# Keeping retention's rotated q on chip, turning y later, storing x1 by halves, and moving part of the last rotations to GpSimd

## The chip, the cores and the metric

The kernel runs on one core of one Trainium2 chip. Its time is the device time of one execution in microseconds (us); the figure for a kernel is the median of several executions. A profile is one more execution, recorded by the hardware; its span runs from the first to the last recorded event, and its own time, taken as for the other runs, is somewhat longer than the span.

The engines are named as in the profile: PE (TensorE, matmuls; PEld is its weight load), DVE (VectorE), ACT (ScalarE), POOL (GpSimd) and SP (SyncE, here only a queue that issues transfers). Each engine works through its instructions strictly in the order in which they were written into its queue, and waits at an instruction until the semaphores it names have come.

## The reference

One layer of a diffusion backbone over 1024 latent tokens (width 1024) with 256 context tokens. One input projection feeds two groups of heads; four heads do bidirectional chunkwise retention, four do differential attention.

```python
h_lat = rms_norm(x, norm1_g) * (1 + sc1) + sh1            # and h_ctx
rq, rk, rv, rg, dq, dk, dv = split(h @ w_in)               # rq, rk, dq, dk of the latents get a rotary embedding
# retention, forward and backward, per head, in chunks of 128
scores = einsum('bhid,bhjd->bhij', qc, kc) * intra
o = einsum('bhij,bhje->bhie', scores, vc) + einsum('bhid,bhde->bhie', qc * q_dec, S)
S = S * c_dec + einsum('bhjd,bhje->bhde', kc * k_dec, vc)
y_ret = silu(rg) * sum over both directions of head_group_norm(o)
# differential attention
a = softmax(s q1 k1) - lam * softmax(s q2 k2);  y_diff = subln(a @ v)
x = x + g1 * (concat([y_ret, y_diff]) @ w_out)
h2 = rms_norm(x, norm2_g) * (1 + sc2) + sh2
x = x + g2 * ((silu(a) * b) @ w_down)                      # a, b = split(conv3(h2 @ w_up))
out = rms_norm(x, final_g)
```

## The kernel before, in words

**Passes.** Every projection product is made of three matmul passes over high and low parts of the operands (`passes`, L131 to L133). The tile `pl` is such a product: 24 matmuls of 128x512, eight steps of three. After each step `tick()` advances a generator that runs beside the projection and writes the instructions of another piece of work between the passes. `beside(gen, rate, start)` sets it: `rate` steps of the generator for each tick, beginning with a debt of `start`.

**Stages.** To about 75 us: modulation vectors, first norm, transposes. Then the column blocks of w_in one after another: dv, dk, retention's v, its k, the silu gate (with the states of heads 0 and 1 beside it), q (block 0, from about 327 us), dq (block 4, eight tiles of 512 columns: two halves `hf` of each of four heads). Beside q and dq runs `outputs()`, which does retention's outputs. The last three dq tiles (`TAIL = 3`) are run beside the first attention units. Attention lasts to about 665 us, the output projection with the second norm to about 755 us, the up and down projections to the end.

**A rotation** (`rotated`, L413 to L426) takes one `pl` tile out of PSUM: ACT writes the two halves of the rows, swapped, to `xb` (L416, two instructions), DVE forms `xa = pl * cos` (L418), `xb = xb * sin` (L419) and `xa = xa + xb` (L420). A q or k tile is then stored to DRAM (L425, `rqk_d`, 256 KB); a dq or dk tile goes through `split_store`: ACT casts the high part (L408), DVE subtracts it for the low part (L409), and a store takes both (L410).

**Retention's outputs.** A `Pair` is two chunks of 128 tokens of one head; there are 16. In iteration n of `outputs()`, pair n + 2 is made, which issues the load of its rotated q and k from DRAM (`qk`, L242, 256 KB). `score` of pair n issues the load of v and the gate (`kvo`, L227), forms q times its decay on POOL (`qq`, L249), and q by k on PE (`pc`, L252, four matmuls); DVE multiplies with the decay mask (`sc`, L254). `output` accumulates `po` on PE from `kvo`, `sc`, the state `S` and `qq` (L260, L261) and ACT copies it out (L265). `squares` takes sums of squares on ACT (L269), POOL a power (L271), DVE scales `o` (L276), POOL adds the directions and multiplies with the gate (`y`, L278, L279: the last reader of `kvo`). `turn` transposes y on PE (`pyt`, L284), ACT and DVE split it (L286, L287) and SP stores it (`yrd`, L289). Pair n is turned in iteration n + 2.

**Entry to attention.** When the last y is done, POOL issues the loads of the first units' queries (`qhl`, L940), keys (`ks`, L943) and values (`va`, L946). A unit's scores `pA` (L861) are reduced by DVE (`mt`, the row minimum, L864), exponentiated by ACT (`p`, L868), combined by DVE (L876) and transposed by PE (`pt`, L881). The steps in `EARLY` of the first two units are set between the passes of the last three dq tiles.

**The output projection** goes over the column halves n = 0, 1 and within each over the eight token tiles t. DVE forms `gated` (L1123) and adds x (L1124). After n = 1, `norm2(t)` stores the sum `x1[t]` to DRAM (`x1d`, L1068, 512 KB), ACT squares it (L1070), and DVE scales it in place (L1074). SP also carries the first loads of w_up (`wra`, `wrb`, L1040) in this stage.

**What sets the order.** The instructions are written in program order as above and a scheduler of the framework then orders each engine's queue; the pools give each tile a number of buffers (`bufs`), and a new tile waits until the last reader of the buffer it takes is done.

Of the kernel before, what the change touches and what calls it, by code (L numbers as in the profile page):

```python
# [8 lines left out]
F32 = mybir.dt.float32  # L9
# [3 lines left out]
ALU = mybir.AluOpType  # L13
# [4 lines left out]
P = 128  # L18
D = 1024
KD = D // P  # L20
L = 1024
# [5 lines left out]
H = 4  # L27
# [5 lines left out]
RET_SCALE = 128.0 ** -0.5  # L33
DIFF_SCALE = 64.0 ** -0.5
# [26 lines left out]
TAIL = 3  # L61
# [6 lines left out]
def r32(ap):  # L68
    return ap.bitcast(F32)
# [3 lines left out]
def kernel(  # L73
# [58 lines left out]
        mm(ps, lh, rl, start=False, stop=False, skip_group_check=more)  # L132
        mm(ps, ll, rh, start=False, stop=last, skip_group_check=more)  # L133

    rqk_d = [dr.tile([P, 2, L], F32, name=f"rqk{h}") for h in range(H)]
    kvg_d = [dr.tile([P, H, 3, 2, P], F32, name=f"kvg{g}") for g in range(NKT // 2)]
    g1_d = dr.tile([P, D], F32, name="g1d")
    g2_d = dr.tile([P, D], F32, name="g2d")
# [15 lines left out]
    with ExitStack() as p1:  # L154
# [68 lines left out]

        def load_kv(h, g, nm, s0):

            kv = rt.tile([P, 2, 2, P], F32, name=nm, bufs=3 + (s0 == 0))
            nc.sync.dma_start(out=kv, in_=kvg_d[g][:, h, s0 : s0 + 2])  # L227
            return kv

# [6 lines left out]
        class Pair:  # L236


            def __init__(self, n):
                self.h, self.g = divmod(n, NT // 2)  # L240
                self.qk = rt.tile([P, 2, 2, P], F32, name="qk")
                nc.sync.dma_start(out=self.qk, in_=rqk_d[self.h][:, :, 2 * self.g * P : (2 * self.g + 2) * P].rearrange("p i (s l) -> p i s l", s=2))  # L242

            def score(self):
                kv = load_kv(self.h, self.g + 1, "kvo", 1)
                self.v, self.sg = kv[:, 0], kv[:, 1]
                over = [P, 2, 2, P]
                self.qq = rt.tile(over, F32, name="qq")
                nc.gpsimd.tensor_tensor(out=self.qq, in0=self.qk[:, 0].unsqueeze(2).to_broadcast(over), in1=qd[:, self.h].unsqueeze(1).to_broadcast(over), op=ALU.mult)  # L249
                pc = tr_tile([P, 2, P], "pc2")  # L250
                for s in range(2):
                    mm(pc[:, s, :], self.qk[:, 1, s, :], self.qk[:, 0, s, :], start=True, stop=True)  # L252
# [38 lines left out]
        states_at, last_y = {}, []  # L291

        def states(heads):

# [43 lines left out]
        def outputs():  # L338
            n_pairs, per_head = H * NT // 2, NT // 2
            pairs, more = {}, states((2, 3))  # L340
            for n in range(-2, n_pairs + 2):
                if n + 2 < n_pairs:
                    pairs[n + 2] = Pair(n + 2)
                if n == -2:
                    continue
                if n + 1 < n_pairs:
                    pairs[n + 1].score()
                forming = per_head <= n < 3 * per_head
                if n == per_head - 1 or forming and n % 2 == 0:
                    next(more)  # L350
                yield
                if 0 <= n < n_pairs:
                    pairs[n].output(0)
                yield
                if forming:
                    next(more)
                yield
                if 0 <= n < n_pairs:
                    pairs[n].output(1)
                    pairs[n].squares()  # L360
                yield
# [40 lines left out]

            return fin

        def split_store(src, dst):
            n = src.shape[-1]
            hl = ev.tile([P, 2, 512], F32R, name="xhl")
            nc.scalar.copy(hl[:, 0, :n], src)  # L408
            nc.vector.tensor_tensor(out=hl[:, 1, :n], in0=src, in1=r32(hl[:, 0, :n]), op=ALU.subtract)  # L409
            nc.sync.dma_start(out=dst.rearrange("p m a l -> (p m) a l"), in_=r32(hl[:, :, :n]))  # L410

        def rotated(pt, dst, rtab, blk, scale, col0, h, hf):
            xa = ev.tile([P, 512], F32, name="xa")  # L413
            xb = ev.tile([P, 512], F32, name="xb")
            for q in (0, 64):
                nc.scalar.activation(xb[q : q + 64, :], pt[64 - q : P - q, :], AF.Copy, scale=scale)  # L416
            cs, sn = rtab[hf][:, 0, :], rtab[hf][:, 1, :]
            nc.vector.scalar_tensor_tensor(out=xa, in0=pt, scalar=scale, in1=cs, op0=ALU.mult, op1=ALU.mult)  # L418
            nc.vector.tensor_tensor(out=xb, in0=xb, in1=sn, op=ALU.mult)  # L419
            nc.vector.tensor_tensor(out=xa, in0=xa, in1=xb, op=ALU.add)  # L420
            c0 = col0 + hf * 512
            if blk == 32:
                split_store(xa, dst[h][:, :, :, c0 : c0 + 512])
            else:
                nc.sync.dma_start(out=dst[h][:, c0 : c0 + 512], in_=xa)  # L425
            return xa  # L426

# [9 lines left out]
        def transposed(wget, dst, rtab, blk, scale, col0, order, nat=False):  # L437
            todo = None
            for h, hf in order:
                pt = mm_tile("pl")  # L440
                for k in range(KD):
                    passes(pt, wget(k, h * P, (h + 1) * P), tuple(hT[a][hf][:, k, :] for a in range(2)), k == 0, k == KD - 1)
                    tick()
                    if todo and k == KD - 2:
                        natural_copy(*todo)
                xa = rotated(pt, dst, rtab, blk, scale, col0, h, hf)
                todo = (xa, h, hf) if nat else None
            if todo:
                natural_copy(*todo)
# [372 lines left out]
        transposed(wg, [q[:, 1] for q in rqk_d], rtab, 64, RET_SCALE, 0, by_head, True)  # L822
        wg = stream_block(3)
        psbS.close()
        psb2 = psx.enter_context(ExitStack())
# [239 lines left out]
        nc.sync.dma_start(out=x1[t], in_=x[t * P : (t + 1) * P, :])  # L1065

    def norm2(t):
        nc.sync.dma_start(out=x1_d[t], in_=x1[t])  # L1068
        sq = xo.tile([P, D], BF16, name="sq2")
        nc.scalar.activation(sq, x1[t], AF.Square, accum_out=sm2[:, t : t + 1])  # L1070
        rsqrt(sm2[:, t : t + 1], sm2[:, t : t + 1], 1.0 / D, EPS, 1)
        if t == 0:
            nc.scalar.activation(sm2[:, 32:33], sm2[:, 0:1], AF.Silu)
        nc.vector.tensor_scalar(out=x1[t], in0=x1[t], scalar1=sm2[:, t : t + 1], scalar2=None, op0=ALU.mult)  # L1074

    def turned(hf, d, raw, on_act):
        pt = pst.tile([P, 512], F32, name="pt3", tag="tr")
# [32 lines left out]
    with ExitStack() as p3:  # L1110
        ps = p3.enter_context(tc.tile_pool(name="ps3", bufs=2, space=PSUM))
        for n in range(2):
            sl = wo_first if n == 0 else []
            for _ in wo_gen if n == 0 else out_weights(n, sl):
                pass
            for t in range(NT):
                pt = ps.tile([P, 512], F32, name="po3", tag="mm")
                for k in range(KD):
                    passes(pt, tuple(yT[a][t // 4][:, k, t % 4 * P : (t % 4 + 1) * P] for a in range(2)), sl[k], k == 0, k == KD - 1)
                    tick()  # L1120
                dst = x1[t][:, n * 512 : (n + 1) * 512]
                gated = wo.tile([P, 512], F32, name="gated")
                nc.vector.tensor_tensor(out=gated, in0=pt, in1=g1[:, n * 512 : (n + 1) * 512], op=ALU.mult)  # L1123
                nc.vector.tensor_tensor(out=dst, in0=gated, in1=dst, op=ALU.add)  # L1124
                if n == 1:
                    norm2(t)
                    if t == 1:
                        pre = [raw_load("wra" if j < 2 else "wrb", w_up[j]) for j in range(NPRE)]
                        early = [[split_op(a[:, c : c + 4, :]) for c in (0, 4)] for a in pre]
                        raws = [up_load(j) for j in range(NSUM)]  # L1130
                        for a, b in raws:
                            sums_in_place(a, b)
                    if t == 3:
                        beside(turned0(), 0.5, -3.0)
        beside(iter(()), 0.0)
# [495 lines left out]
```

## Time and the profile before

| | |
|---|---|
| median of 3 runs | 1394.26 us (1393.91 to 1397.99) |
| profiled execution: its own time | 1398.66 us |
| profiled execution: span | 1396.9 us |
| mean granted clock of PE | 0.997 |
| busy in the span | PE 1365.7 us (98%), DVE 1003.0 (72%), ACT 729.6 (52%), POOL 296.9 (21%) |
| chain that ended last | PE 86%, DMA 5%, DVE 4%, ACT 2%, issue 2%, POOL 1% |

The page of the profile lists busy time by engine, the span in 40 slices of about 35 us, the transfers, the chain of work that ended last, and the costliest groups of instructions. The waits view lists for an engine the instruction that waited, the one that released it, the sum in us, the count and the longest. In a timeline row the numbers are the start, the duration, the engine, line and operation, and in square brackets the idle time of the engine before it and what ended it.

### The profile page before, as it was taken

Reading aid. Unit: us, or ns where it says so; the run is one execution under the profiler, and the core shown is the slowest. Engines: PE = TensorE matmul, PEld = TensorE weight load, DVE = VectorE, ACT = ScalarE, POOL = GpSimd, SP = SyncE. Lnnn points to the kernel's source line nnn. Section 1 sums busy time; section 2 is a strip of 40 time slices with the busy share of each in tenths; the row PEclk is TensorE's granted clock in tenths of the full one; section 3 lists DMA queues with packets and bytes.
Section 4 is the critical chain, followed back from the end, with each engine's and each line's share of the span. In section 5 each row is a group of like instructions: output and inputs, shape, how many; then the busy total and the mean of one; then the engine's idle time right before and its main releaser. Section 6 shows DMA issues by size and latency. Waiting matters only on the chain.

```text
span 1396.9 us, 19447 instructions
## 1 busy us (share of the span) xinstructions
PE 1365.7 (98%) x7038; PEld 1146.9 (82%) x7038; DVE 1003.0 (72%) x1462; ACT 729.6 (52%) x1395; POOL 296.9 (21%) x321
## 2 busy tenths in 40 slices
PE   8999999999999899999999999999999999999997
PEld 5788888888887799998888788888888888888886
DVE  4655773424676798896347998777788777798757
ACT  4652222424575689997126645555445555454543
POOL 1310000001556133421201732233332220000001
PEclk9999999999999999999999999999999999999999
DMA  9546885465574696641421223323233225963523
GB/s 360 211 166 216 286 277 175 142 174 164 178 237 141 181 222 155 127 97 46 166 84 61 91 106 114 113 91 113 100 111 113 85 81 177 374 232 99 181 91 128
DMA packets 96807, 218.81 MB, mean 157 GB/s; under 512 B 9220, under 2 KB 31236, under 8 KB 96200
## 3 DMA queue, kind: packets, MB, share of 16 engines
q1 hardware_dynamic: 87976, 190.83, 40.0%
q0 software_dynamic: 8160, 24.91, 7.9%
q10 hardware_dynamic: 576, 1.84, 0.4%
q8 instruction: 55, 0.90, 0.3%
q14 instruction: 40, 0.33, 0.1%
HBM read 160.13 MB, written 57.41 MB: 156 GB/s over the span
## 4 chain that ended last, share of the span: by engine, by line
PE 86%; DMA 5%; DVE 4%; ACT 2%; issue 2%; POOL 1%; SPq 0%; POOLq 0%; ACTq 0%; DVEq 0%
PE chain L131 5%; PE chain L133 5%; PE chain L132 5%; PE pv L893 5%; PE c L132 5%; PE pA L861 5%; PE c L131 5%; PE c L133 5%; PE pn L131 4%; PE pn L133 4%; PE pn L132 4%; PE pl L133 3%; PE pl L131 3%; PE pl L132 3%; PE third L131 3%; PE third L133 3%
## 5 line engine op out<-in xcount | busy, mean ns | idle before, releaser
L131 PE MATMUL pl<-hT,whi 128*128 128x512 f32 x256 | 106.5, 416 | 0.0
L131 PE MATMUL chain<-T,whi 128*128 128x512 f32 x264 | 103.2, 392 | 0.7 <-ACT ua L1177 0.4
L132 PE MATMUL chain<-T,whi 128*128 128x512 f32 x264 | 102.8, 389 | 0.0
L133 PE MATMUL chain<-T,wlo 128*128 128x512 f32 x264 | 102.4, 389 | 0.0
L133 PE MATMUL pl<-hT,wlo 128*128 128x512 f32 x256 | 100.6, 393 | 0.0
L132 PE MATMUL pl<-hT,whi 128*128 128x512 f32 x256 | 100.4, 392 | 0.0
L864 DVE TENSOR_REDUCE mt<-pA 128x1 f32<-128x1280 f32 x64 | 95.3, 1490 | 3.7 <-PE pA L861 3.3
L861 PE MATMUL pA<-ks,qhl 128*128 128x512 f32 (+1 forms) x384 | 89.5, 369 | 3.0 <-ACT p L868 2.7
L133 PE MATMUL c<-whi,ghl 128*128 128x512 f32 x232 | 90.3, 389 | 0.0
L131 PE MATMUL c<-whi,ghl 128*128 128x512 f32 x232 | 90.3, 389 | 0.0
L132 PE MATMUL c<-wlo,ghl 128*128 128x512 f32 x232 | 90.3, 389 | 0.0
L868 ACT ACTIVATE p<-pA,mt 128x1280 f32<-128x1280 f32 x64 | 85.5, 1335 | 6.8 <-DVE mt L864 6.7
L1032 ACT CAST whi<-cmb 128x512 fp32r<-128x512 f32 x62 | 38.5, 622 | 81.1 <-PE chain L132 60.7
L861 PEld LDWEIGHTS pA<-ks,qhl 128*128 128x128 f32 x384 | 67.6, 189 | 15.2 <-ACT p L868 3.4
L893 PE MATMUL pv<-va,aT 128*128 128x128 f32 x640 | 76.9, 275 | 0.1
L131 PE MATMUL pn<-whi,hT 128*128 128x512 f32 x188 | 76.8, 409 | 0.0
L133 PE MATMUL pn<-whi,hT 128*128 128x512 f32 x188 | 73.8, 393 | 1.3 <-POOL hT L548 1.2
L1035 DVE TENSOR_TENSOR wlo<-cmb,whi 128x512 fp32r<-128x512 f32 x62 | 60.3, 974 | 20.3 <-ACT whi L1032 20.3
L1191 POOL TENSOR_TENSOR cmb<-wrb 128x512 f32<-128x512 f32 x19 | 27.8, 1462 | 221.1 <-DMA wrb<-w_up 132.0
L893 PEld LDWEIGHTS pv<-va,aT 128*128 128x128 f32 x640 | 74.0, 192 | 0.7 <-DVE yT L922 0.3
L132 PE MATMUL pn<-wlo,hT 128*128 128x512 f32 x188 | 73.7, 392 | 0.8 <-DVE wlo L571 0.8
L1032 ACT CAST whi<-wra 128x512 fp32r<-128x512 f32 x55 | 33.7, 622 | 72.8 <-PE third L132 42.5
(319 smaller groups left out, 3822.5 us busy)
## 6 DMA issues: line engine op xcount, KB each, us to landing
wm<-w_mod SPq DMA_DIRECT2D x32, 512.0 KB, 5.3
raw<-w_in SPq DMA_DIRECT2D x27, 512.0 KB, 4.6
wra<-w_up SPq DMA_DIRECT2D x24, 512.0 KB, 3.3
wrb<-w_up SPq DMA_DIRECT2D x22, 512.0 KB, 3.6
W<-w_down SPq DMA_DIRECT2D x44, 256.0 KB, 5.3
ad<-s SPq DMA_DIRECT2D x20, 512.0 KB, 3.5
wra<-ad SPq DMA_DIRECT2D x20, 512.0 KB, 3.7
kvs<-kvg SPq DMA_DIRECT2D x36, 256.0 KB, 3.1
```

Of the source, the lines that this page charges most:

```text
L131: mm(ps, lh, rh, start=first, stop=False, skip_group_check=more)
L132: mm(ps, lh, rl, start=False, stop=False, skip_group_check=more)
L133: mm(ps, ll, rh, start=False, stop=last, skip_group_check=more)
L861: mm(self.pa[m][:, c0:c1], self.q[:, m, i, qs], self.k[:, m, c0:c1], start=(i == 0), stop=(i == 1))
L864: nc.vector.tensor_reduce(out=self.mt[:, m : m + 1], in_=self.pa[m][:, :LK], axis=AX.X, op=ALU.min)
L868: nc.scalar.activation(self.p[m], self.pa[m][:, :LK], AF.Exp, scale=-1.0, bias=self.mt[:, m : m + 1], accum_out=self.s[:, m : m + 1])
L893: mm(self.pv, self.aT[:, c, :], self.v[:, c, :], start=(c == 0), stop=(c == NKT - 1))
L1032: cast = nc.scalar.copy(hi, src)
L1035: nc.vector.tensor_tensor(out=lo, in0=src, in1=r32(hi), op=ALU.subtract)
L1191: nc.gpsimd.tensor_tensor(out=s1, in0=b1, in1=b2, op=ALU.add)
```

## The change

Four edits are made together.

1. **q stays in SBUF.** `rotated` is called with no destination for block 0. The result stays in its tile (`turned_q[h, hf]`: an `st` buffer for the first half of a head, the `xa` buffer for the second), and `score` reads q from there. The eight q stores of 256 KB are gone. What a pair loads is k alone (`rk`, 128 KB in place of `qk`, 256 KB). The `kvo` load moves from `score` to the making of the pair, two pairs earlier, and `kvo` has four buffers, not three.
2. **y is turned in iteration n + 3**, in the middle of the iteration, not n + 2 at its end. The loop is one iteration longer, and the start debt is 16 rather than 18.
3. **x1 is stored by halves** of 512 columns, each right after its own add, and the scaling of the second norm is done as two instructions of 512 columns.
4. **In the last three dq tiles** the product with the sine and the low-part subtraction run on POOL.

```diff
-    rqk_d = [dr.tile([P, 2, L], F32, name=f"rqk{h}") for h in range(H)]
+    rk_d = [dr.tile([P, L], F32, name=f"rk{h}") for h in range(H)]
...
-            kv = rt.tile([P, 2, 2, P], F32, name=nm, bufs=3 + (s0 == 0))
+            kv = rt.tile([P, 2, 2, P], F32, name=nm, bufs=4)
...
-                self.qk = rt.tile([P, 2, 2, P], F32, name="qk")
-                nc.sync.dma_start(out=self.qk, in_=rqk_d[self.h][:, :, 2 * self.g * P : (2 * self.g + 2) * P]...)
-
-            def score(self):
+                self.k = rt.tile([P, 2, P], F32, name="rk")
+                nc.sync.dma_start(out=self.k, in_=rk_d[self.h][:, 2 * self.g * P : (2 * self.g + 2) * P]...)
                 kv = load_kv(self.h, self.g + 1, "kvo", 1)
                 self.v, self.sg = kv[:, 0], kv[:, 1]
+
+            def score(self):
+                o = self.g % 2 * 2 * P
+                q = turned_q[self.h, self.g // 2][:, o : o + 2 * P].rearrange("p (s l) -> p s l", s=2)
...
-                    mm(pc[:, s, :], self.qk[:, 1, s, :], self.qk[:, 0, s, :], start=True, stop=True)
+                    mm(pc[:, s, :], self.k[:, s, :], q[:, s, :], start=True, stop=True)
...
-            for n in range(-2, n_pairs + 2):
+            for n in range(-2, n_pairs + 3):
...
+                if 0 <= n - 3 < n_pairs:
+                    pairs[n - 3].turn()
                 if 0 <= n < n_pairs:
                     pairs[n].output(1)
...
-                if 0 <= n - 2 < n_pairs:
-                    pairs[n - 2].turn()
                 yield
...
-            nc.vector.tensor_tensor(out=hl[:, 1, :n], in0=src, in1=r32(hl[:, 0, :n]), op=ALU.subtract)
+            eng.tensor_tensor(out=hl[:, 1, :n], in0=src, in1=r32(hl[:, 0, :n]), op=ALU.subtract)
...
-            xa = ev.tile([P, 512], F32, name="xa")
+            if dst is None and hf == 0:
+                xa = ev.tile([P, 4, P], F32, name="st").rearrange("p h e -> p (h e)")
+            else:
+                xa = ev.tile([P, 512], F32, name="xa")
+            if dst is None:
+                turned_q[h, hf] = xa
...
-            nc.vector.tensor_tensor(out=xb, in0=xb, in1=sn, op=ALU.mult)
+            eng.tensor_tensor(out=xb, in0=xb, in1=sn, op=ALU.mult)
             nc.vector.tensor_tensor(out=xa, in0=xa, in1=xb, op=ALU.add)
...
-        beside(outputs(), 1.35, -18.0)
-        transposed(wg, [q[:, 0] for q in rqk_d], rtab, 64, 1.0, 0, by_head)
+        beside(outputs(), 1.35, -16.0)
+        transposed(wg, None, rtab, 64, 1.0, 0, by_head)
...
-        transposed(wg, dq_d, rtab, 32, -DIFF_SCALE, 0, by_head[-TAIL:])
+        transposed(wg, dq_d, rtab, 32, -DIFF_SCALE, 0, by_head[-TAIL:], eng=nc.gpsimd)
...
     def norm2(t):
-        nc.sync.dma_start(out=x1_d[t], in_=x1[t])
...
-        nc.vector.tensor_scalar(out=x1[t], in0=x1[t], scalar1=sm2[:, t : t + 1], scalar2=None, op0=ALU.mult)
+        for c in (0, 512):
+            nc.vector.tensor_scalar(out=x1[t][:, c : c + 512], in0=x1[t][:, c : c + 512], scalar1=sm2[:, t : t + 1], scalar2=None, op0=ALU.mult)
...
                 nc.vector.tensor_tensor(out=dst, in0=gated, in1=dst, op=ALU.add)
+                nc.sync.dma_start(out=x1_d[t][:, n * 512 : (n + 1) * 512], in_=dst)
```

In the changed kernel the same code has other line numbers: the load of k is L242, the score matmuls `pc` are L254, `po` L262 and L263, the rotation L425 to L427, the subtraction L411, `mt` L871, the store of x1 L1132, the loads of w_up L1047.

The first scores of retention on PE, before: two `pc` of two pairs and all eight `po` of a pair stand close together, 61 `pl` passes into block 0.

```order
L131 MATMUL pl<-hT_167,whi 128x512
L252 MATMUL pc_2925<-qk 128x128 x2
L132 MATMUL pl<-hT_169,whi 128x512
L133 MATMUL pl<-hT_167,wlo 128x512
L252 MATMUL pc_2957<-qk 128x128 x2
L260 MATMUL po<-kvo,sc 128x128
L261 MATMUL po<-S_2463,qq 128x128
L260 MATMUL po<-kvo,sc 128x128
L261 MATMUL po<-S_2464,qq 128x128
L260 MATMUL po<-kvo,sc 128x128
```

The same place on PE after; `st` is the kept q. The upper piece is the first `pc`, the lower one begins 13 passes behind it.

```order
L133 MATMUL pl<-hT_170,wlo 128x512
L254 MATMUL pc_2920<-st,rk 128x128 x2
...
L133 MATMUL pl<-hT_167,wlo 128x512
L254 MATMUL pc_2954<-st,rk 128x128 x2
L262 MATMUL po<-kvo,sc 128x128
L263 MATMUL po<-S_2463,qq 128x128
L262 MATMUL po<-kvo,sc 128x128
L263 MATMUL po<-S_2464,qq 128x128
L131 MATMUL pl<-hT_167,whi 128x512
```

The first `pc` now stands 39 passes into block 0 (15 behind the end of the first q tile), the second 15 passes later, and the eight `po` are in two groups with six passes between them.

On DVE at the entry to attention, before: the rotations of the last dq tiles with the reductions `mt` of the first units between them.

```order
L419 TENSOR_TENSOR xb<-xb,rtab_3723 128x512
L864 TENSOR_REDUCE mt<-pA 128x1
L420 TENSOR_TENSOR xa<-xa,xb 128x512
L872 RECIPROCAL r<-sa 128x1
L409 TENSOR_TENSOR xhl<-xa,xhl 128x512
L864 TENSOR_REDUCE mt<-pA 128x1 x2
L873 SCALAR_TENSOR_TENSOR r<-r,sa,nlam 128x1
L876 SCALAR_TENSOR_TENSOR p_4275<-p_4273,r,p_4275 128x1280
L864 TENSOR_REDUCE mt<-pA 128x1
```

On DVE after:

```order
L425 SCALAR_TENSOR_TENSOR xa<-pl,rtab_3740 128x512
L871 TENSOR_REDUCE mt<-pA 128x1
L879 RECIPROCAL r<-sa 128x1
L427 TENSOR_TENSOR xa<-xa,xb 128x512
L425 SCALAR_TENSOR_TENSOR xa<-pl,rtab_3739 128x512
L871 TENSOR_REDUCE mt<-pA 128x1 x2
L427 TENSOR_TENSOR xa<-xa,xb 128x512
L880 SCALAR_TENSOR_TENSOR r<-r,sa,nlam 128x1
L883 SCALAR_TENSOR_TENSOR p_4267<-p_4265,r,p_4267 128x1280
L871 TENSOR_REDUCE mt<-pA 128x1
```

The product with the sine (before L419) and the subtraction (before L409) of these tiles have left DVE. They stand on POOL, behind the loads of the first units; on POOL after:

```order
L953 DMA va<-dvd 128x10x128
L426 TENSOR_TENSOR xb<-xb,rtab_3740 128x512
L947 DMA qhl<-dq_85 64x4x512
L411 TENSOR_TENSOR xhl<-xa,xhl 128x512
L426 TENSOR_TENSOR xb<-xb,rtab_3739 128x512
L947 DMA qhl<-dq_85 64x4x512
L411 TENSOR_TENSOR xhl<-xa,xhl 128x512
```

So L427 on DVE waits for L426 on POOL, and the reductions queued behind L427 on DVE wait with it.

On SP in the output projection the order after is as follows; before, no `x1d` stood ahead of these loads of `wra` and `wrb`, and all eight came as whole tiles behind `woraw`.

```order
L1132 DMA x1d_94<-x_0_6682 128x512
L1047 DMA wrb<-w_up 128x1024
L1132 DMA x1d_95<-x_1_6683 128x512
L1047 DMA wra<-w_up 128x1024
L1047 DMA wrb<-w_up 128x1024
L1047 DMA wra<-w_up 128x1024
L1132 DMA x1d_96<-x_2_6684 128x512
L1047 DMA wrb<-w_up 128x1024
```

More of the change, by code (lines that the diff above doesn't have):

```diff
@@ L289, in turn @@
                 nc.sync.dma_start(out=yr_d[self.g // 2][:, :, self.h, o : o + 2 * P].rearrange("p a (s l) -> p a s l", s=2), in_=r32(yr))
-        states_at, last_y = {}, []
+        states_at, last_y, turned_q = {}, [], {}
         def states(heads):
@@ L403, in store_to, with split_store @@
             return fin
-        def split_store(src, dst):
+        def split_store(src, dst, eng=nc.vector):
             n = src.shape[-1]
@@ L408, in split_store, with rotated @@
             nc.scalar.copy(hl[:, 0, :n], src)
-            nc.vector.tensor_tensor(out=hl[:, 1, :n], in0=src, in1=r32(hl[:, 0, :n]), op=ALU.subtract)
+            eng.tensor_tensor(out=hl[:, 1, :n], in0=src, in1=r32(hl[:, 0, :n]), op=ALU.subtract)
             nc.sync.dma_start(out=dst.rearrange("p m a l -> (p m) a l"), in_=r32(hl[:, :, :n]))
-        def rotated(pt, dst, rtab, blk, scale, col0, h, hf):
-            xa = ev.tile([P, 512], F32, name="xa")
+        def rotated(pt, dst, rtab, blk, scale, col0, h, hf, eng=nc.vector):
+            if dst is None and hf == 0:
[4 more added lines that the diff above has]
+                turned_q[h, hf] = xa
             xb = ev.tile([P, 512], F32, name="xb")
@@ L422, in rotated @@
             if blk == 32:
-                split_store(xa, dst[h][:, :, :, c0 : c0 + 512])
-            else:
+                split_store(xa, dst[h][:, :, :, c0 : c0 + 512], eng)
+            elif dst is not None:
                 nc.sync.dma_start(out=dst[h][:, c0 : c0 + 512], in_=xa)
@@ L435, in natural_copy, with transposed @@
                 nc.sync.dma_start(out=kvg_d[1 + 2 * hf + i][:, h, 0], in_=st[:, 2 * i : 2 * i + 2, :])
-        def transposed(wget, dst, rtab, blk, scale, col0, order, nat=False):
+        def transposed(wget, dst, rtab, blk, scale, col0, order, nat=False, eng=nc.vector):
             todo = None
@@ L445, in transposed @@
                         natural_copy(*todo)
-                xa = rotated(pt, dst, rtab, blk, scale, col0, h, hf)
+                xa = rotated(pt, dst, rtab, blk, scale, col0, h, hf, eng)
                 todo = (xa, h, hf) if nat else None
@@ L821 @@
         rt = rtx.enter_context(tc.tile_pool(name="rt", bufs=2, side="right"))
-        transposed(wg, [q[:, 1] for q in rqk_d], rtab, 64, RET_SCALE, 0, by_head, True)
+        transposed(wg, rk_d, rtab, 64, RET_SCALE, 0, by_head, True)
         wg = stream_block(3)
```

4 lines of the change are left out of this document (2 added, 2 removed).

## The prediction

> **What bounds the kernel now.** I read the summary of busy time first, then the list of waits for PE, then the busy time stage by stage, and last the chain and the timeline at the few places where PE stood still.
>
> ```profile
> PE 1365.7 (98%) x7038; PEld 1146.9 (82%) x7038; DVE 1003.0 (72%) x1462; ACT 729.6 (52%) x1395; POOL 296.9 (21%) x321
> ```
>
> PE works for 98% of the span, so the only time to be had without removing matmuls is its idle time, 1396.9 - 1365.7 = 31.2 us. The change removes no matmul. The waits of PE (sum in us, count, longest) tell which part of those 31 us it can reach:
>
> ```profile
> PE pc L252 <- DMA qk<-rqk: 4.5, 3, 1.6
> PE pA L861 <- ACT p L868: 2.7, 2, 1.7
> PE po L260 <- DMA kvo<-kvg: 1.9, 1, 1.9
> ...
> PE pu L326 <- ACT jk L269: 1.0, 1, 1.0
> ...
> PE pt L881 <- DVE xa L418: 0.9, 1, 0.9
> PE pyt L284 <- POOL y L279: 0.4, 1, 0.4
> PE pA L861 <- DMA ks<-dk: 0.3, 1, 0.3
> ```
>
> All seven lie in retention and at the entry to attention. By stage (stretch, length, busy time of PE, PEld, DVE, ACT, POOL, then the granted clock):
>
> ```profile
> 350.00:400.00 50.00, 46.85 (x314) 41.98 (x313) 34.06 (x80) 30.89 (x101) 27.44 (x30) 1.00 0.65 204
> 400.00:450.00 50.00, 46.15 (x269) 39.47 (x268) 35.63 (x77) 28.97 (x96) 29.20 (x31) 0.97 0.52 171
> 450.00:500.00 50.00, 46.10 (x263) 39.37 (x263) 38.21 (x50) 32.14 (x62) 11.91 (x23) 1.00 0.78 187
> ...
> 700.00:800.00 100.00, 99.26 (x466) 80.91 (x465) 73.44 (x115) 54.00 (x89) 28.46 (x17) 1.00 0.22 82
> 800.00:1300.00 500.00, 500.00 (x2204) 412.95 (x2203) 412.40 (x493) 260.41 (x382) 106.97 (x79) 1.00 0.39 135
> ```
>
> From 350 to 500 us PE idles 10.9 us, nowhere behind it does it idle as much: from 800 to 1300 it has no idle time at all, and what is saved ahead of it moves the end by as much.
>
> **The q kept in SBUF.** The chain shows how q reaches PE before:
>
> ```profile
> 331.18 2.53 DMA rqk<-xa
> 333.72 3.87 DMA qk<-rqk
> 337.63 0.71 PE pc L252 x4
> ...
> 351.06 3.76 DMA qk<-rqk
> ...
> 363.50 5.69 DMA qk<-rqk
> 369.32 0.68 PE pc L252 x4
> ```
>
> A store of 2.5 us and a load of 3.8 to 5.7 us stand between the rotation and the scores, and the three waits of `pc` are these loads. Afterwards `pc` needs a tile that DVE has just written and a `rk` that was stored long before (k is rotated two column blocks earlier). The 4.5 us go. What is late next is the rotation itself:
>
> ```profile
> 333.36 1.20 ACT L416 ACTIVATE xb<-pl 64x512 f32<-64x512 f32 x2 [4.26 <-PE pl L133]
> 334.59 0.69 DVE L418 SCALAR_TENSOR_TENSOR xa<-pl,rtab 128x512 f32<-128x512 f32 x1 [3.44 <-ACT xb L416]
> ...
> 335.92 0.69 DVE L420 TENSOR_TENSOR xa<-xa,xb 128x512 f32<-128x512 f32 x1
> ...
> 331.12 0.39 PE L131 MATMUL pl<-hT,whi 128*128 128x512 f32 x1
> 331.35 0.39 PE L132 MATMUL pl<-hT,whi 128*128 128x512 f32 x1
> ```
>
> From the end of the product to the rotated tile it takes 336.61 - 333.36 = 3.25 us. In the new order 15 passes stand between the end of the first q tile and the first `pc`; passes start 331.35 - 331.12 = 0.23 us apart, so they cover 3.4 us, some 0.2 us less than rotation and two handovers at most. I put the new wait at 0.2 us, its ends at 0 and 0.7 (one DVE instruction late). Later pairs have several tiles' time. The balance of this part is -4.5 + 0.2 = -4.3 us.
>
> **The earlier load of v and gate, and the clock.** At 427 us SP stands at the `kvo` load, because its buffer is read by `y` of an earlier pair on POOL, and PE stands behind it:
>
> ```profile
> 427.45 4.39 SPq L227 DMA_DIRECT2D kvo<-kvg  x2
> ...
> 431.31 0.46 PE L260 MATMUL po<-kvo,sc 128*128 128x128 f32 x2 [1.89 <-DMA kvo<-kvg]
> ...
> 432.70:436.10 3.40, 3.40 (x13) 3.03 (x12) 2.32 (x6) 0.90 (x2) 1.48 (x3) 0.50 0.43 149
> 436.10:440.00 3.90, 3.90 (x23) 3.32 (x22) 1.62 (x3) 2.28 (x11) 2.78 (x3) 1.00 0.38 146
> ```
>
> Issued two iterations ahead and into a fourth buffer, the load has two iterations to land: eighteen iterations share the time from the first `pc` at 337 us to the entry to attention at about 450, 6 us each, so 12 us in all. The 1.9 us go. Right behind the stall PE ran for 3.4 us at a granted clock of 0.50. Its 13 matmuls took 3.40 us where 23 took 3.90 us afterwards; that costs between 3.40 - 13 x 0.17 = 1.2 us and half of 3.40 = 1.7 us, and I take 1.5. It follows the longest pause of the stage, and I assume that it goes with the pause. [...]
>
> **The turn three iterations on.** The wait of `pyt` for `y` is 0.4 us and goes, since y has one more iteration to be done. The number of matmuls stays. The same work on POOL, ACT and DVE stands in other places of the row, with less time between a score and its output; as a new wait I take one like the 1.0 us of `pu` behind `jk`: +1.0, ends 0 and 3 (three such).
>
> **The entry to attention.** Four waits, 1.73 + 0.93 + 0.97 + 0.26 = 3.9 us:
>
> ```profile
> 466.45 0.62 ACT L408 CAST xhl<-xa 128x512 fp32r<-128x512 f32 x1 [2.06 <-DMA dq<-xhl]
> 467.10 0.69 DVE L409 TENSOR_TENSOR xhl<-xa,xhl 128x512 fp32r<-128x512 f32 x1 [2.51 <-ACT xhl L408]
> ...
> 467.71 2.88 DVE L864 TENSOR_REDUCE mt<-pA 128x1 f32<-128x1280 f32 x2
> ...
> 470.75 1.43 PE L861 MATMUL pA<-ks,qhl 128*128 128x512 f32 x6 [1.73 <-ACT p L868]
> ...
> 482.46 1.43 PE L861 MATMUL pA<-ks,qhl 128*128 128x512 f32 x6 [0.97 <-ACT p L868]
> L1191 POOL TENSOR_TENSOR cmb<-wrb 128x512 f32<-128x512 f32 x19 | 27.8, 1462 | 221.1 <-DMA wrb<-w_up 132.0 <-DMA ad<-tconv 36.4 <-DVE wlo L1035 26.2
> ```
>
> The first is plain: the cast waits for the buffer of an earlier `dq` store, the subtraction on DVE waits for the cast, and two `mt` reductions wait behind the subtraction on DVE, though they don't need it. With the subtraction on POOL the reductions come up to 2.5 us earlier and the 1.73 us go. The loads of the first unit are issued 53 passes ahead of its first scores, not 46: 7 x 0.23 = 1.6 us more, so the 0.26 goes. Against that, L427 on DVE now waits for POOL's L426, 1.46 us (the nearest POOL row of this shape) in place of 0.69, three times, with reductions behind it: 3 x 0.77 = 2.3 us of lateness, of which passes between cover part. So the gain lies between 3.9 and 3.9 - 2.3 = 1.6 us, or nothing where more of POOL's lateness shows. I take 2.0.
>
> [...] The rows first (minimum, median, longest in ns, and a single POOL instruction):
>
> ```profile
> L419 DVE TENSOR_TENSOR xb<-xb,rtab x32: 678/681/1749, 104.5 to 478.9; 128x512 f32<-128x512 f32 x32
> L418 DVE SCALAR_TENSOR_TENSOR xa<-pl,rtab x32: 667/691/694, 103.9 to 478.3; 128x512 f32<-128x512 f32 x32
> L1191 POOL TENSOR_TENSOR cmb<-x 128x512 f32<-128x512 f32 x1 | 13.2, 13167 | 18.1 <-DVE yT L1087 18.1
> ```
>
> L419, two operands in SBUF, stretches by up to 1.07 us; L418, one operand in PSUM, never. [...]
>
> **x1 by halves.** DVE waits for the stores in the second norm, PE does not: it is busy 99.26 of 100 us there, so the gain is at most 0.7 us. The loss: SP reaches some loads of w_up later, behind a store that waits for an add.
>
> ```profile
> DVE x L1074 <- DMA x1d<-x: 6.4, 5, 1.3
> 678.48 0.33 SPq L1040 DMA_DIRECT2D wrb<-w_up  x1
> ```
>
> The last of these early loads is issued at 678 us, 77 us ahead of the up projection at 755; some 5 us more are hidden. One more DVE instruction per token tile costs nothing while it waits anyway. I take 0, ends -0.7 and +0.7.
>
> **The sum**, against the profiled execution's own 1398.66: -4.3 - 1.9 - 1.5 - 0.4 + 1.0 - 2.0 + 0 = -9.1, that is 1389.6. The median of the three runs is 1394.26, 4.4 us under the profiled execution. If its runs hold the same waits, -9.1 gives 1385.2; if the half clock is an accident of the profiled one, -7.6 gives 1386.7. I say 1386.0.
>
> **The rivals.**
>
> *The waits change their names.* PE still meets late work in retention (SP holds `rk` behind a `kvo` that waits for POOL) and at the entry POOL gives back what DVE gains. For it speaks that SP already spends long at that place:
>
> ```profile
> SPq L227 <- POOL y L279: 27.6, 12, 4.2
> ```
>
> Against it, that a wait of 4.2 us is less than the 12 us by which the load now comes earlier. Then about 3 of the 9.1 us remain: 1391.3, with some of it under and some over 1390.1.
>
> [...]
>
> *The change does little.* The waits of a profiled run are not those of a usual one, and the 4.4 us between them are already the saved part: then 1394.26 - 9.1 + 4.4 = 1389.6 to 1394, about 1392.
>
> **How the numbers follow.** A measurement of this kernel can tell about 0.3%, 4.2 us: faster is below 1390.1, slower above 1398.4. Chances: forecast 0.60 (all under 1390.1), changed names 0.20 (half under, half within), little 0.10 (within, a little under), lock 0.10 (slower). So faster 0.60 + 0.10 + 0.03 = 0.73, within 0.17, slower 0.10. The low end of the range takes everything: 4.5 + 1.9 + 1.7 + 0.4 + 3.9 + 0.7 = 13.1, so 1381.2; the high end reaches into the second and third case, 1392.5. What lies outside is the lock and the upper edge of these, under 2 in 10.
>
> **What would show it right or wrong.** Right: in the waits of PE no `pc` behind a load of q or k, no `po` behind `kvo`, PE over 48 of 50 us from 350 to 450 us, granted clock 1.00 there; at the entry the sum of waits 1 to 2.5 us. Wrong: `pc` or `po` waiting for `rk` or `kvo`; a row of L426 or L411 on POOL over 2 us with DVE L427 waiting for it and PE `pA` behind; PE waits in the output projection or at the start of the up projection.

## The result, and the profile after

The changed kernel takes 1390.81 us (median of 6 runs, 1389.03 to 1391.29) against 1394.31 us (6 runs, 1393.84 to 1397.99): ratio 0.9966, 95% interval 0.9955 to 0.9977, so 4.7 us less by the ratio, 3.2 to 6.3. In a later set of runs (e11) it was 0.9966 again (0.9953 to 0.9979). The forecast was 1386.0 with a range of 1381.2 to 1392.5: the side and the range hold, and the gain is a little over half of the 8.3 us that were forecast. The line that the forecast drew between faster and within, 1390.1, lies between the median and what the ratio gives (1389.6).

The waits of PE in the changed kernel (sum in us, count, longest):

```profile
PE pyt L286 <- POOL y L281: 1.6, 1, 1.6
...
PE pt L1086 <- DVE x L1081: 1.3, 1, 1.3
...
PE pu L328 <- ACT jk L271: 1.1, 1, 1.1
PE pt L888 <- DVE xa L425: 0.9, 1, 0.9
PE chain L131 <- ACT ub L1293: 0.8, 1, 0.8
...
PE pA L868 <- ACT p L875: 0.3, 1, 0.3
```

No `pc` waits for a load, no `po` for `kvo`, and the waits at the entry are down to 0.9 + 0.3. In their place stand a wait of the last `pyt` for `y`, and two that weren't there before: `pt` for x in the second norm and `chain` for `ub` in the up projection. The busy time by stage (stretch, length, PE, PEld, DVE, ACT, POOL, granted clock):

```profile
350.00:400.00 50.00, 50.00 (x341) 45.30 (x340) 35.21 (x86) 35.34 (x115) 31.87 (x32) 1.00 0.56 172
400.00:450.00 50.00, 47.19 (x268) 40.19 (x267) 32.26 (x70) 27.56 (x87) 29.43 (x34) 1.00 0.50 155
450.00:500.00 50.00, 48.68 (x303) 42.04 (x302) 40.52 (x52) 39.42 (x78) 18.51 (x28) 1.00 0.83 216
```

PE idles 4.1 us from 350 to 500 us where it idled 10.9. That is more than the runs gained, so two things had to be found: what in the first profile of the kernel before isn't in its usual execution, and what was given back behind 500 us.

For that the profiles are compared by stage, from the first `pl` of the projections, since what lies ahead of it varies by 2 us between the profiles (the first `pl` starts at 92.87 to 95.03 us). Each number is the difference of two starts in the timeline: to the last `pyt` (retention), on to the first `pty` (entry to attention), to the first `chain` (attention and output projection), to the first `c` (up projection), to the end. With the new turn the last `pyt` stands six `pl` passes further back in PE's row (684 passes ahead of it, 678 with the old turn; in e7 687). Six passes are 1.4 us (0.23 us each), so between kernels with different turns that much of the first column belongs to the second; the sum isn't affected.

| profile of | retention | entry | attention, output | up | to the end | sum |
|---|---|---|---|---|---|---|
| before, first | 355.08 | 44.87 | 259.53 | 419.46 | 224.02 | 1302.96 |
| before, again (e1) | 351.22 | 44.49 | 259.58 | 419.47 | 224.06 | 1298.82 |
| changed | 348.58 | 41.80 | 259.65 | 420.71 | 225.36 | 1296.10 |
| changed, again (e11) | 348.14 | 41.94 | 259.64 | 420.71 | 225.67 | 1296.10 |
| q alone (e2) | 348.46 | 43.74 | 259.67 | 419.50 | 224.08 | 1295.45 |
| q, late kvo (e10) | 347.55 | 44.19 | 259.88 | 419.47 | 224.04 | 1295.13 |
| q and POOL (e5) | 347.15 | 42.07 | 259.56 | 419.51 | 224.96 | 1293.25 |
| changed without halves (e3) | 348.36 | 41.52 | 259.65 | 419.44 | 224.15 | 1293.12 |
| the same again (e12) | 347.54 | 41.50 | 259.62 | 419.49 | 225.43 | 1293.58 |
| changed, late turn without halves (e7) | 347.25 | 50.51 | 259.62 | 419.44 | 224.02 | 1300.84 |
| changed without POOL (e4) | 347.25 | 49.46 | 259.88 | 420.72 | 225.20 | 1302.51 |
| POOL alone (e8) | 351.90 | 41.85 | 259.89 | 419.43 | 224.06 | 1297.13 |
| halves alone (e9) | 352.06 | 45.78 | 259.57 | 420.69 | 224.13 | 1302.23 |
| halves, one scaling (e6) | 347.80 | 42.27 | 259.62 | 422.02 | 224.08 | 1295.79 |

### The profile page after: what moved, and what is told of

Its sections match the earlier page's. It is cut to its first block, busy times and chain, and to the rows that moved or that the text cites. A ratio compares the mean times of both kernels' runs of the same rounds, so it can differ in the third digit from the quotient of the medians.

```text
span 1389.5 us, 19442 instructions
## 1 busy us (share of the span) xinstructions
PE 1363.6 (98%) x7038; PEld 1145.9 (82%) x7038; DVE 996.3 (72%) x1464; ACT 731.9 (53%) x1395; POOL 306.2 (22%) x327
## 5 line engine op out<-in xcount | busy, mean ns | idle before, releaser
L871 DVE TENSOR_REDUCE mt<-pA 128x1 f32<-128x1280 f32 x64 | 95.1, 1490 | 3.7 <-PE pA L868 2.3
L868 PEld LDWEIGHTS pA<-ks,qhl 128*128 128x128 f32 x384 | 67.7, 189 | 12.7 <-ACT p L875 1.0
```

Of the source, the lines that this page charges most:

```text
L868: mm(self.pa[m][:, c0:c1], self.q[:, m, i, qs], self.k[:, m, c0:c1], start=(i == 0), stop=(i == 1))
L871: nc.vector.tensor_reduce(out=self.mt[:, m : m + 1], in_=self.pa[m][:, :LK], axis=AX.X, op=ALU.min)
```

## The experiments

The theory after the result: the gain lies in retention and at the entry, the first profile of the kernel before overstates it, and the halves give some back. The rivals: the waits only changed their names, or all of the first profile's waits are in every execution and the loss lies elsewhere.

**The kernel before once more (e1).** Its edit: none.

> The kernel before once more, for a second profile. Theory A (part of the 7.4 us between the two profiles is an accident of the first profile of before, which was 4.3 us above its median): ratio 1.000, and the profile shows a time of 1393.5 to 1395 us, without the stretch at half clock at 433 us (1.5 us) and with some of the waits behind qk and kvo smaller. Theory B (the waits are in every execution, and the changed kernel loses time elsewhere): the profile shows the half clock and the 1.9 us wait for kvo again, and a time near 1398.

Ratio 0.9993 (0.9984 to 1.0001). The profiled execution took 1393.47 us, the lowest of its eleven (to 1396.91). Waits of PE, and the stretch that held the half clock in the first profile:

```profile
PE pc L252 <- DMA qk<-rqk: 3.8, 3, 1.5
PE pA L861 <- ACT p L868: 2.9, 2, 1.9
PE po L260 <- DMA kvo<-kvg: 1.9, 1, 1.9
...
PE pyt L284 <- POOL y L279: 0.5, 1, 0.5
...
400.00:450.00 50.00, 47.56 (x283) 40.78 (x281) 34.93 (x77) 30.00 (x96) 31.24 (x37) 1.00 0.59 179
```

The pause for `kvo` is the same, 1.9 us, but the clock stays at 1.00 behind it. Retention is 3.86 us shorter than in the first profile: some 1.5 of half clock, 1.6 of two `pu` waits, 0.7 of `pc`. Theory A holds: these differ from one execution to the next, and the waits of `pc`, `kvo` and the entry are in both.

**q alone (e2), and q without the early kvo (e10).** e2 is the changed kernel with the old turn, x1 whole and the rotations on DVE. e10 is e2 with this on top:

```diff
-            kv = rt.tile([P, 2, 2, P], F32, name=nm, bufs=4)
+            kv = rt.tile([P, 2, 2, P], F32, name=nm, bufs=3 + (s0 == 0))
...
-                kv = load_kv(self.h, self.g + 1, "kvo", 1)     # in Pair.__init__
...
+                kv = load_kv(self.h, self.g + 1, "kvo", 1)     # in score
```

> Edit 1 alone: q kept in SBUF, kvo issued with the pair into four buffers; the turn, x1 and the last rotations as before. Theory 1 (the gain lies in retention): -4.5 of pc and -1.9 of kvo in the profile, no pc behind rk; measured against before 3 to 5 us faster. Theory 2 (the waits change their names): pc or po wait elsewhere in retention and it is less than 2 us faster.

> q kept in SBUF alone, with the load of v and gate where it was before, in score and with three buffers. Theory 1 (the load of kvo is a wait of its own): the 1.9 us wait of po for kvo is back, 1.5 to 2 us slower than q alone (0.9957), ratio 0.997 to 0.998; if the pause costs clock, half clock shows behind it. Theory 2 (without the q stores and loads on SP the load of kvo is no longer late): within 0.5 us of q alone.

e2: 0.9957 (0.9944 to 0.9969). e10: 0.9964 (0.9953 to 0.9976). The waits of PE in e2:

```profile
PE pyt L286 <- POOL y L281: 2.0, 2, 1.7
PE po L262 <- DVE S L336: 1.7, 1, 1.7
PE pA L868 <- ACT p L875: 1.6, 2, 1.0
```

and in e10:

```profile
PE po L262 <- DVE yr L289: 1.7, 1, 1.7
PE po L262 <- DVE S L336: 1.7, 1, 1.7
...
PE pA L868 <- ACT p L875: 1.3, 2, 1.0
```

`pc` no longer waits in either, and q alone is worth 6 us by its ratio, more than the 3 to 5 that I had expected, and 3.4 by the two profiles (1298.82 - 1295.45). In e10 the first wait, at 424.66 us, stands where that for `kvo` stood, three us behind the last `pc`; only the name of what came last differs. In e2 it is gone, and the last `pyt` waits 1.7 us for `y` instead, 0.6 in e10. Retention is not shorter in e2 than in e10 (348.46 against 347.55). So the early load takes away a wait that comes back some us later. I read it so: behind the last scores PE is ahead of the chain over ACT, POOL and DVE that ends in `y`, and has to wait for it somewhere. The profiles differ by 0.3 us in sum, the ratios by 1.0 with intervals that overlap; theory 2 of e10 fits.

**Without the POOL part (e4), and the POOL part alone (e8).** e4 is the changed kernel with `eng=nc.gpsimd` taken out; e8 is the kernel before with edit 4.

> The changed kernel with the last three rotations wholly on DVE, as before. Theory 1 (the POOL part frees the reductions behind the subtraction): the waits of pA for the exponentials at the entry to attention come back, 2 to 2.7 us of the 3.9, and it is 2 to 3 us slower than the changed kernel. Theory 2 (the entry was helped by the earlier loads alone): within 0.7 us of the changed kernel.

> The kernel before with edit 4 alone: the last three rotations partly on POOL. Theory 1 (freeing the reductions is worth its waits in any order): the waits of pA for the exponentials fall from 2.7 to 2.9 us to under 0.7, ratio 0.998 to 0.9985. Theory 2 (the part on POOL pays only for the new order, in which rotations and reductions stand closer): ratio 0.9995 or above.

e4: 1.0027 (1.0016 to 1.0037), slower than the kernel before, and 6.4 us by the profiles (1302.51 against 1296.10), over twice what I had expected. e8: 0.9983 (0.9973 to 0.9993); its entry takes 41.85 us against 44.49, as expected. In e4, the waits of PE, the timeline at the first and at the third of the subtractions, the busy time of that stage and of two stretches in it:

```profile
PE pA L868 <- ACT p L875: 5.9, 2, 3.9
...
455.68 0.62 ACT L410 CAST xhl<-xa 128x512 fp32r<-128x512 f32 x1 [3.43 <-DMA dq<-xhl]
456.33 0.69 DVE L411 TENSOR_TENSOR xhl<-xa,xhl 128x512 fp32r<-128x512 f32 x1 [2.03 <-ACT xhl L410]
456.94 1.49 DVE L871 TENSOR_REDUCE mt<-pA 128x1 f32<-128x1280 f32 x1
...
459.93 1.59 PE L868 MATMUL pA<-ks,qhl 128*128 128x512 f32 x6 [1.98 <-ACT p L875]
...
473.21 0.68 DVE L411 TENSOR_TENSOR xhl<-xa,xhl 128x512 fp32r<-128x512 f32 x1
473.81 2.88 DVE L871 TENSOR_REDUCE mt<-pA 128x1 f32<-128x1280 f32 x2
...
476.79 1.43 PE L868 MATMUL pA<-ks,qhl 128*128 128x512 f32 x6 [3.91 <-ACT p L875]
...
450.00:500.00 50.00, 43.17 (x251) 38.05 (x251) 37.85 (x49) 33.28 (x65) 8.54 (x17) 0.93 0.71 187
...
461.00:464.30 3.30, 3.30 (x10) 2.64 (x9) 3.17 (x3) 1.08 (x2) 0.00 (x0) 0.50 0.24 91
478.00:481.60 3.60, 3.60 (x20) 3.60 (x20) 3.20 (x4) 2.81 (x5) 2.20 (x4) 0.53 0.57 180
```

and at the first subtraction in the changed kernel:

```profile
454.36 1.40 PE L868 MATMUL pA<-ks,qhl 128*128 128x512 f32 x6
...
455.79 1.49 DVE L871 TENSOR_REDUCE mt<-pA 128x1 f32<-128x1280 f32 x1 [0.91 <-PE pA L868]
...
460.60 2.88 DVE L871 TENSOR_REDUCE mt<-pA 128x1 f32<-128x1280 f32 x2
460.68 1.30 POOL L411 TENSOR_TENSOR xhl<-xa,xhl 128x512 fp32r<-128x512 f32 x1 [4.50 <-ACT xhl L410]
...
463.64 1.43 PE L868 MATMUL pA<-ks,qhl 128*128 128x512 f32 x6
```

With the subtraction on DVE the reductions stand behind it, the exponential behind them and PE behind that, 3.9 us in one wait and 5.9 in two. Behind each of the two pauses PE ran at about half clock for over 3 us (0.50 in 3.30 us, 0.53 in 3.60 us). With the subtraction on POOL the first reduction starts as soon as its scores are done, and the next two run beside the subtraction. In the old order (e1) the same waits are 2.9 us.

So the edit is worth 2.6 us at the entry in the old order and 7.7 us in the new one (49.46 - 41.80). Of the 7.7, 5.5 are idle time of PE (6.8 against 1.3 us) and the rest are slower rows at half clock (0.50 and 0.53 in the two stretches above; a `pl` row there took 0.63 us, and 0.39 where the clock is 1.00). Why the entry without the edit is so much worse in the new order isn't shown. It isn't the earlier end of retention: e2 and e10 have that too, and their entries are 43.74 and 44.19 us. What e4 has beside them is the new turn and the halves, and the halves alone lengthen the entry by about 1 us (45.78 in e9).

**The turn (e5, e7).** e5 is q and the POOL part with the old turn and x1 whole, to be held against e3 (the same with the new turn). e7 is e3 with the turn two steps later:

```diff
                 yield
-                if 0 <= n - 3 < n_pairs:
-                    pairs[n - 3].turn()
                 if 0 <= n < n_pairs:
                     pairs[n].output(1)
...
                 yield
+                if 0 <= n - 3 < n_pairs:
+                    pairs[n - 3].turn()
                 yield
```

> Edits 1 and 4 together; the turn at n + 2 with the start debt of 18 and x1 whole, as before. Against q alone (ratio 0.9957) and against the changed kernel without the halves (0.9941), which has the new turn besides. Theory 1 (the POOL part saves its 2 to 2.8 us of waits at the entry whatever the turn): 0.994, level with the kernel without the halves, so the new turn is worth nothing by itself. Theory 2 (the new turn carries its own gain in retention): 0.9957 to 0.996, 2 us slower than without the halves.

> The changed kernel without the halves, and the turn of pair n - 3 at the end of the iteration, two steps later. Theory 1 (the wait of the last pyt for y, 1.6 us, is a wait for work two steps of the side generator early, 2 steps by 1.35 a tick by 0.68 us = 1.0 us): that wait falls to about 0.6 us and the kernel is 0.5 to 1 us faster than without the halves, 0.9935. Theory 2 (y itself moves with it, or the loads of attention behind it come later by as much): the same as without the halves, 0.994, or up to 1 us slower.

e5: 0.9961 (0.9945 to 0.9977). That is the ratio of theory 2, and the 0.994 of theory 1 lies just outside; but the kernel without the halves measured 0.9941 and 0.9950 in its two sets (e3, e12), with intervals that overlap that of e5. By the profiles its stages sum to 1293.25 against 1293.12 and 1293.58 for e3 and e12. So the ratios lean to a gain of the new turn and the profiles to none; that it gains anything isn't shown. e7: 0.9997 (0.9988 to 1.0007), some 7 us slower than e3, where I had expected a gain or at most 1 us of loss. What PE waited for, and the timeline:

```profile
PE pl L131 <- DVE xa L425: 5.9, 1, 5.9
...
445.62 14.02 SPq L291 DMA_DIRECT2D yrd<-yr  x2
458.27 0.37 ACT L288 CAST yr<-pyt 128x256 fp32r<-128x256 f32 x1 [11.91 <-DMA yrd<-yr]
461.16 0.80 PE L131 MATMUL pl<-hT,whi 128*128 128x512 f32 x1 [5.94 <-DVE xa L425]
```

The wait of `pyt` fell to 0.3 us as expected. But a store of `yr` now went out at 445.6 us, behind the loads of attention (POOL issues `qhl` from 441.7 us and `ks` from 444.2), and its buffer came free 12.7 us later. `yr` has one buffer, so the next cast on ACT waited 11.9 us, with the rotation of a dq tile behind it and PE behind that. In the changed kernel the last store of `yr`, issued at 448.0 us, took 11.3 us too, but no turn comes behind it. So the earlier turn, with its wait of 1.6 us, is ahead of these loads where it matters.

**The halves (e3, e6, e9).** e3 is the changed kernel with x1 stored and scaled whole. e6 keeps the stores by halves and scales whole. e9 is the kernel before with edit 3 alone.

> The changed kernel with x1 stored whole and scaled whole, as before. Theory 1 (the scaling by halves put a transposition of x ahead of a DVE row that POOL stretched to 1.48 us): the wait of pt for x (1.3 us at 748 us) is gone and it is 1 to 1.5 us faster than the changed kernel, 1389.5 against 1390.8. Theory 2 (the stores by halves save DVE waits that matter): it is 1 us slower than the changed kernel.

> The changed kernel with x1 stored by halves, but scaled in one instruction of 1024 columns. Theory 1 (the halves cost by the split scaling, whose place on DVE puts a transposition behind a row that POOL stretches): the 1.3 us wait of pt for x is gone and the time falls by 1.3 to 2 us of the 3.5 by which the kernel without halves is faster. Theory 2 (the cost sits in the stores and in what SP issues): within 0.5 us of the changed kernel.

> The kernel before with edit 3 alone. Theory 1 (the halves let the scheduler set the transposition of the last token tile earlier in PE's row, where it waits for the second norm, and add DVE rows): a wait of pt for x of about 1.3 us and waits of chain of 0.5 us more, ratio 1.001 to 1.0025. Theory 2 (the cost is only there in the changed kernel): 0.9995 to 1.0005.

e3: 0.9941 (0.9929 to 0.9953). e6: 0.9970 (0.9959 to 0.9981). e9: 1.0015 (1.0006 to 1.0023). The halves cost time wherever they are, in the stage of the up projection: 420.7 us with them, 419.5 without, in all thirteen profiles that have both or neither part of them. In the changed kernel:

```profile
745.48 0.49 PE L1086 MATMUL pt<-ident,x 128*128 128x128 f32 x3
...
747.08 1.27 POOL L1196 TENSOR_TENSOR cmb<-wrb,wra 128x512 f32<-128x512 f32 x1
747.15 1.48 DVE L1081 TENSOR_SCALAR x<-x,sm 128x512 f32<-128x512 f32 x1 [0.67 <-POOL sm L114]
...
748.69 0.33 PE L1086 MATMUL pt<-ident,x 128*128 128x128 f32 x1 [1.32 <-DVE x L1081]
```

and in e3:

```profile
746.83 1.29 POOL L1195 TENSOR_TENSOR cmb<-wrb,wra 128x512 f32<-128x512 f32 x1
746.88 1.79 DVE L1042 TENSOR_TENSOR wlo<-wrb,whi 128x512 fp32r<-128x512 f32 x1 [0.64 <-ACT whi L1039]
...
748.59 0.75 DVE L1081 TENSOR_SCALAR x<-x,sm 128x1024 f32<-128x1024 f32 x1
...
749.59 0.38 PE L1086 MATMUL pt<-ident,x 128*128 128x128 f32 x2
```

The last token tile can't be transposed before its norm. With x1 whole, its two first transpositions stand 22 rows behind that of tile 4 in PE's row, and the scaling is done; with the halves the scheduler sets the first of them 9 rows behind, and PE arrives 1.3 us early. On DVE the scaling by halves took the place ahead of a weight's low part, started while POOL worked, and took 1.48 us where its like takes 0.49; in e3 the low part came first and took 1.79 us beside POOL (in the changed kernel the median of this row is 0.69). Taking only the split away (e6) doesn't mend it: the stores by halves alone keep the wait (1.0 us) and add others, 422.0 us in this stage. So theory 1 of e3 and e9 holds in place and size, but not in its cause, the split scaling. By the profiles e6 is within 0.5 us of the changed kernel, as its theory 2 had it; how the stores bring the transposition forward isn't shown.

**The changed kernel and e3 on one chip (e11, e12).**

> The changed kernel once more, on the chip of the next one. Expected 0.9966, with the same waits (pyt 1.6, pt for x 1.3, pu 1.1) and the last load of a weight landing 4.3 us after its issue, if that belongs to the program; 2.5 to 3 us, and an end 1.3 us earlier, if it was an accident of one execution.

> The changed kernel without the halves, beside the changed kernel on one chip. Expected 2.5 to 3.5 us faster than the changed kernel, 0.994 of the kernel before, if the halves cost what the profiles show (1.3 at pt, 0.4 at chain, 1.3 at the end); under 1 us if the difference came from the chip.

e11: 1390.33 us, 0.9966 (0.9953 to 0.9979). e12: 1388.97 us, 0.9950 (0.9938 to 0.9962). The version without the halves beats both kernels, in both of its sets. On this chip the difference to the changed kernel is 1.4 us, less than the 2.5 to 3.5 that I had expected and about the 1.25 of the up stage, and the intervals overlap. The last 1.3 us of the changed kernel's profile, from the first `c` to the end, are not the halves': e3 and e12 are one kernel and end 224.15 and 225.43 us behind it. The last load of that stage, in e3 and in e12 (line, KB, us to landing):

```profile
wra<-ad SPq DMA_DIRECT2D x1, 256.0 KB, 3.0
wra<-ad SPq DMA_DIRECT2D x1, 256.0 KB, 4.3
```

In the changed kernel it is late in both profiles too, and DVE carries the delay to the end:

```profile
1354.50 0.32 SPq L1370 DMA_DIRECT2D wra<-ad  x1
1358.76 0.62 ACT L1039 CAST whi<-wra 128x512 fp32r<-128x512 f32 x1 [2.58 <-DMA wra<-ad]
1359.41 0.69 DVE L1042 TENSOR_TENSOR wlo<-wra,whi 128x512 fp32r<-128x512 f32 x1 [1.37 <-ACT whi L1039]
```

Why the load takes 2.5 to 3.0 us in ten of the profiles and 4.0 to 4.6 in four (the changed kernel twice, e4, e12) stays open.

## Why the prediction was right, and where its terms were not

**The side.** PE was the bound, and what was taken off its waits ahead of 500 us moved the end. Against the second profile of the kernel before, the changed kernel gains 2.64 us in retention and 2.69 at the entry (4.0 and 1.3 with the six passes counted in one stage), and gives 1.24 back in the up projection and 1.30 at the end: 2.7 us in sum, with an execution of the kernel before that was its fastest. The runs say 4.7 (3.2 to 6.3). Where the other 2 us lie is argued, not shown. Retention of the kernel before differs by 3.9 us between two profiles, that of the changed kernel by 0.4, so the usual execution of before may lose more there. But the second profile also has the earliest start of the first `pl` of all fourteen, 92.87 us against 93.11 to 95.03. And the granted clock plays a part: of the 67 runs of the kernel before in the three later sets that took under 1400 us, the 33 with a mean of 0.998 or more took 1395.0 us on average, the 34 below that 1397.6. The runs don't tell where in the execution the clock was lost. In the profiles, from 300 to 500 us, it was lost in retention once (the first of before, 0.97 from 400 to 450 us) and behind the long pauses of e4 and e7 (0.93 from 450 to 500 us); in the other eleven it is 1.00 there.

The median was 4.8 us above the forecast, and the range of 11 us held it. The largest term that was too big is retention: -5.6 without the half clock, where the idle time of PE fell by 3.3 us (7.2 in e1, 3.9 in the changed kernel).

**pc: -4.5 + 0.2.** Right. 3.8 and 4.5 us in the two profiles before, none after; the first `pc`, 15 passes behind its tile, didn't wait.

**kvo: -1.9.** The step "the load has two iterations to land" was right, and the wait went, but the question of what is late next was not asked there. It was `y` of the last pair: 1.6 us at the last `pyt`. By e10 the early load gains nothing that shows, with the old turn.

**The half clock: -1.5.** The step that took it for a sure part of the pause failed. The same 1.9 us pause left the clock at 1.00 in e1, and so did two others of 1.9 us (in e1 and e9). But a pause of 2.0 us in e4 was followed by 3.3 us at 0.50, one of 3.9 us (e4) by 3.6 us at 0.53, and behind the 5.9 us of e7 a `pl` row took 0.63 us, where it takes 0.39 at a clock of 1.00. From 300 to 500 us three of the fourteen profiles were below 1.00 (before, e4, e7); the half clock shown in them stands behind a pause of 1.9 us or more, and not every such pause is followed by one. So the reading 1386.7, that it is an accident of the execution, was the better one. What sets the half clock isn't shown.

**pyt: -0.4.** Wrong in sign: 0.4 became 1.6, although the turn came later. It is the term in which the kvo gain came back. The +1.0 for a new wait has no row of its own: `pu` behind `jk` waits 1.1 us in the changed kernel and 0.7 in e11, but it waited 1.0 in the first profile of before and not in the second.

**The entry: -2.0.** In idle time of PE it is -2.5 (3.8 us in e1, 1.3 in the changed kernel), and -2.6 for edit 4 alone (e8 against e1), between its ends of 0 and 3.9. The mechanism was the one named: the reductions no longer stand behind the subtraction. What I hadn't seen is that the other edits without edit 4 make the entry 5 us longer (49.46 against 44.49). The lateness of L426 on POOL didn't come: all six POOL rows there (L426, L411) took 1.27 to 1.37 us. The 0.10 for a lock that makes the kernel slower was an estimate of mine, and no run shows one. What PE still waits at the entry is the 0.9 and 0.3 us shown above, of which the 0.9 was there before.

**x1 by halves: 0, ends -0.7 and 0.7.** Too narrow: +1.25 by the profiles, +2.1 (0.8 to 3.2) alone by its ratio. I had looked at SP, where no wait of PE came from, and not at PE's row, where the scheduler moved a transposition ahead of its norm.

**The rivals.** "The waits change their names" came true in part: of 6.2 us of `pc`, `kvo` and `pyt` (second profile of before), 2.7 are left as waits of `pyt` and `pu` (2.3 in e11). "The change does little" had the reason right that the first profile of before was not its usual execution.

**The signs.** Of the signs of being right all came but one: PE was busy 47.2 of the 50 us from 400 us, not over 48. One of the signs of being wrong came as well: a wait of PE at the start of the up projection, 1.3 us of `pt` at 748.7 us.

## What to carry to other kernels

Profile a kernel twice before summing its waits: here 3.9 us of the first profile's retention, waits and half clock, were gone in the second. When a wait of the bounding engine is taken away, follow that engine to the next point where it needs the same chain of work, and price that wait too: here 1.9 us of `kvo` came back as 1.6 us of `pyt`. An edit on one engine can change the order in which the scheduler sets the bounding engine's row; look there, not only on the engine that was edited. And count the passes ahead of a mark before comparing stages: an edit that moves the mark moves time from one stage to the other.

## What the runs showed of the hardware

A DVE scaling of 128x512 in place, with one operand in SBUF, took 0.49 us in the median of its 16, and once 1.48 us in the changed kernel and once in e9; in e4 and e11 the wait of `pt` for it is 1.3 us as in these two. In the changed kernel the long one stood beside a POOL instruction of 1.27 us that ended 0.3 us before it. No run here varies that POOL instruction alone.

A store of 256 KB (`yrd`), 3.5 us to landing in the median of the profile of before, took 11.3 us in the changed kernel when it was issued behind the loads of attention, and in e7 such a store kept its buffer for 12.7 us and PE waited 5.9 us behind it: in this kernel the store that frees the only buffer of its tile is better not issued behind these loads.
